# Sums of weighed ada chunks folded on VectorE over 32x32 block transposes, and copies of the bias rows issued from Pool's queue in the first MLP

## The chip, the cores and the metric

The kernel runs on one core of a Trainium2 chip. The metric is the device time of one execution in microseconds (us), as the median over runs. PE is TensorE, DVE is VectorE, ACT is ScalarE, POOL is GpSimd, and SP is SyncE, which here only issues DMAs.

## What is computed

Two transformer layers act on 256 latent tokens `x` and 256 context tokens `ctx`, with width D = 1024. Layer 0 mixes tokens by retention (4 heads, both directions, a gate per head), layer 1 by neighbourhood attention with a relative position bias `rpb`; each is followed by an MLP with squared ReLU and 4096 hidden units. Each layer takes six modulation vectors from the conditioning vectors `c` (latent) and `c_ctx` (context):

```
mod   = silu(c)    @ ada_w[i] + ada_b[i]       # 6 x 1024 numbers
mod_c = silu(c_ctx) @ ada_w[i] + ada_b[i]
sh1, sc1, g1, sh2, sc2, g2 = split(mod, 6)
h = x * (1 + sc1) + sh1                        # shift and scale, before each mixer and MLP
x = layer_norm(alpha * x + g1 * mixer(h))      # g: the gate on the branch
```

All data are 32-bit floats. The matrix `ada_w` has 2 x 1024 x 6144 elements, so the products are small beside the rest, but their weights are 48 MB.

## The kernel before

**The big products** are three matmuls each: ACT rounds a weight chunk `raw` to `hi`, DVE makes `lo = raw - hi`, activations are split in the same way (`hTh`/`hTl`, `oh`/`ol`), and PE adds `hi*hi + lo*hi + hi*lo` in PSUM. Weight chunks of 512 KB come over SP's queue into a ring of four buffers. Results are named after their stage: `pq`, `pv`, `pS`, `pg`, `pw` are the projections, scores, gates and output products of the retention heads, and `p` those of the MLPs and of layer 1.

**The retention heads** run one after the other (h = 0 to 3). The last stage of a head multiplies its gated output by the output weights: for each half of the columns and for each of four token tiles, 12 matmuls into `pw`. Each token tile is turned by PE, copied by ACT into `oh`, and its remainder `ol` is made by DVE (`to_oT`), two tiles ahead of the stage's first half and two within it. DVE then makes `acc = pw * G`, and POOL or DVE adds `acc` to the residual `R`. Scratch tiles (`acc`, `far`, `neg` and others) come from one ring of eight buffers, `scr`.

**The modulation vectors** for later use come from a background stream, the generator `bg_stream` (line 508). It goes through ten parts of `ada_w` (layer, which half of the layer w, and part 0 and 1 for shift and scale, 2 for the gate), with eight chunks (n = 0 to 7) of 512 KB for each part, called `rawa`. A call of `bg()` at certain places of the retention heads and of the MLPs advances the stream by one chunk, and loads the chunk after it into the same ring of four buffers that the weights use. The first part goes through PE. For the other nine, DVE weighs the rows (`weigh`, line 479): the element of silu(c) on each partition times the chunk, added up over chunks in `strips` (layer 0: 128x512 for each of latent and context) or `acc` (layer 1: 128x1024). What is left is a sum over the 128 partitions:

- `fold_rows` (line 488) adds the partitions up on PE: matmuls of 256 columns with a weight tile of 32 columns (`onecol`, in tile `misc`) that holds a column of ones, so that the sums land in one row of a group of 32 partitions. Layer 0 does so six times (in two halves for each of three parts, for latent and context), layer 1 six times (two with latent and context, four with latent alone).
- `ada_row` (line 445) adds the bias, which two DMAs on SP's queue (`ada_bias`, line 422) have spread over the partitions in `brow`.
- For shift and scale, `ada_columns` (line 451) turns the row into columns with two matmuls against the constant `sel`, and DVE writes them to `mods` with two adds. This is deferred to the next call of `bg()` by the list `due`. For the gate, POOL writes the row to DRAM (`grow`), from where it is later read on all partitions.

**The bias rows** of layer 1: `outside` (line 380) stores the negated bias in DRAM (`rpb_neg`) and fills the DRAM array `rpb_rows` with a large number by 14 DMAs of 256 KB (`far`) on SP's queue. `shifted_biases` (line 391) then copies for each of 64 grid columns a window of 16 columns from `rpb_neg` into `rpb_rows`, in 79 DMAs on SP's queue. They are read by POOL's DMAs in layer 1's attention. `outside` is called in head 2 of the retention.

**What sets the order**: a tile scheduler places the instructions of an engine by their dependences and priorities; each engine then runs its list strictly in order, and an instruction that waits holds all that stand behind it.

Of the kernel before, what the change touches and what calls it, by code (L numbers as in the profile page):

```python
# [39 lines left out]
def make_consts():  # L40
    f = np.float32
    parts = []

    def add(name, a):
        off = sum(p.shape[1] for p in parts)
        CONST_COLS[name] = (off, a.shape[1])
        parts.append(a.astype(f))

    p = np.arange(P)
    add("ident", np.eye(P))  # L50
    sel = np.zeros((P, 8))
    for j in range(4):
        for i in range(2):
            sel[32 * j + i, 2 * j + i] = 1.0
    add("sel", sel)

    sel4 = np.zeros((P, 4))
    for j in range(4):
        for i in range(2):
            sel4[32 * j + i, i] = 1.0  # L60
    add("sel4", sel4)
    inv = f(1.0) / (f(10000.0) ** (np.arange(0, 128, 2, dtype=f) / f(128.0)))
    row = np.arange(NLAT // GRID_W).astype(f)
    col = np.arange(GRID_W).astype(f)
    inv2 = inv[p % 64]
    for nm, ax in (("row", row), ("col", col)):
        ang = (ax[None, :] * inv2[:, None]).astype(f)
        add("cos" + nm, np.cos(ang))
        sg = np.where(p < 64, 1.0, -1.0)[:, None]
        add("sin" + nm, np.sin(ang) * sg)  # L70
    base = np.concatenate(parts, axis=1)
    d = (np.arange(384)[None, :] - 128 - p[:, None]).astype(f)
    return np.ascontiguousarray(base, dtype=f), np.ascontiguousarray(d)
# [36 lines left out]
def kernel(  # L110
# [184 lines left out]

    NC0 = P + 8 + 4
# [18 lines left out]
    cT = cpool.tile([P, KC, 16, 2], F32, tag="cT", name="cT")  # L317
    scol = cpool.tile([P, 2, KC], F32, tag="scol", name="scol")
    bcol = cpool.tile([P, 2, KC], F32, tag="bcol", name="bcol")
    lns = dram.tile([64, P], F32, tag="lns", name="lns")  # L320

    def first_columns():
# [16 lines left out]
    def ln_rows():  # L339
        rows = scr("rows")[:, :P]  # L340
        sp.dma_start(out=rows[0:32, :], in_=ln_g.rearrange("l i (k p) -> (l i k) p", p=P))
        sp.dma_start(out=rows[32:64, :], in_=ln_b.rearrange("l i (k p) -> (l i k) p", p=P))
        return rows

    def ln_columns(rows):

        pc = bank("pc")
        pe.transpose(pc[:, 0:64], rows[0:64, :], ident[0:64, 0:64])
        dve.tensor_copy(out=lnT[:].rearrange("p a b c k -> p (a b c k)"), in_=pc[:, 0:64])
        lsc = scr("lsc")  # L350
        pool.tensor_scalar_mul(out=lsc[0:64, :P], in0=rows[0:64, :], scalar1=ALPHA)
        pool.dma_start(out=lns[:], in_=lsc[0:64, :P])
# [38 lines left out]
    def shifted_biases(q):  # L391
        cs = min(max(q - 8, 0), GRID_W - 16)
        for b in range(2):
            c0, c1 = max(cs, HALFW * b), min(cs + 16, HALFW * (b + 1))
            if c0 < c1:
                src = rpb_neg[:, 4 : 4 + NRR, 15 - q + c0 : 15 - q + c1]
                sp.dma_start(out=rpb_rows[q][:, b, :, c0 - HALFW * b : c1 - HALFW * b], in_=src)


    pool.memset(onecol[:], 0.0)  # L400
# [19 lines left out]
        return raw  # L420

    def ada_bias(l, offs, nb):
        brow = smp.tile([P, 256], F32, tag="brow", name=nm("brow"), bufs=1)
# [24 lines left out]
        dve.tensor_add(out=row[p0:p1, :nb], in0=pr[p0:p1, 0:nb], in1=brow[p0:p1, :nb])  # L448
        return row

    def ada_columns(l, w, pr, row, nb, c0):

        ni = nb // P
        for i in range(ni):
            pe.matmul(
                pr[:, 256 + 8 * i : 264 + 8 * i],
                lhsT=row[:, i * P : (i + 1) * P],
                rhs=cv("sel"),
                start=True,
                stop=True,  # L460
            )
        m = mods[l, w]
        for s in range(2):
            src = pr[:, 256 : 256 + 8 * ni].rearrange("p (i s j t) -> p s j i t", i=ni, s=2, j=2)[:, s]
            dst = m[:, s, c0 : c0 + 2 * ni, :].rearrange("p (j i) t -> p j i t", i=ni)
            dve.tensor_scalar_add(out=dst, in0=src, scalar1=float(s))

    def on_pe(l, w, part):
        return (l, w, part) == (0, 0, 2)
# [10 lines left out]
    def weigh(acc, raw, t, k, first):  # L480
# [7 lines left out]
    def fold_rows(pr, js, nt, src):  # L488

        for t in range(nt):  # L490
            for i, j in enumerate(js):
                pe.matmul(
                    pr[32 * j : 32 * j + 32, 0:256],
                    lhsT=onecol[:, 1 - t : 33 - t],
                    rhs=src(t)[:, i * 256 : (i + 1) * 256],
                    start=(t == 0),
                    stop=(t == nt - 1),
                    tile_position=(0, 32 * j),
                )


    due = []

# [4 lines left out]
    def bg_stream():  # L508


        plan = []
        for l, w, part in (
            [(0, 0, 2), (0, 1, 0), (0, 1, 1), (0, 1, 2)]
            + [(1, 0, 0), (1, 0, 1), (1, 0, 2), (1, 1, 0), (1, 1, 1), (1, 1, 2)]
        ):
            sh, sc, g = 3 * w * D, (3 * w + 1) * D, (3 * w + 2) * D
            offs = (sh + 512 * part, sc + 512 * part) if part < 2 else (g, g + 512)
            for n in range(KC):
                plan.append((l, w, part, offs, n))
        nxt = bg_load(*plan[0])  # L520
        yield
        for step, (l, w, part, offs, n) in enumerate(plan):
            raw = nxt
            if step + 1 < len(plan):
                nxt = bg_load(*plan[step + 1])

            nt = 2 if l == 0 or (w == 0 and part < 2) else 1
            if n == 0:
                brow = ada_bias(l, offs, 256)
                row = None  # L530
            if on_pe(l, w, part):
                if n == 0:
                    pr = bank("pada")
                ada_mm(pr, n, 256, lambda j: raw[:, j // 2, (j % 2) * 256 : (j % 2 + 1) * 256])
                if n == KC - 1:
                    row = ada_row(pr, brow, 256)
            elif l == 0:
                for kk in range(2):
                    for t in range(nt):
                        weigh(spare(t), raw[:, kk, :], t, 2 * (n % 4) + kk, n % 4 == 0 and kk == 0)  # L540
                if n % 4 == 3:
                    yield
                    s = n // 4
                    pr = bank("pada")
                    fold_rows(pr, (2 * s, 2 * s + 1), nt, spare)
                    row = ada_row(pr, brow, 256, 64 * s, 64 * s + 64, row)
            else:
                if n == 0:
                    acc = slot(S_VL, [P, 2, D], F32, "acc")
                for t in range(nt):  # L550

                    dve.on = n == 0 and (w, part) == (0, 0)
                    weigh(acc[:, t], raw[:].rearrange("p a n -> p (a n)"), t, n, n == 0)
                    dve.on = False
                if n == KC - 1:
                    pr = bank("pada")
                    fold_rows(pr, range(4), nt, lambda t: acc[:, t])
                    row = ada_row(pr, brow, 256)
            if n == KC - 1:
                if part < 2:  # L560
                    due.append(lambda a=(l, w, pr, row, 256, 4 * part): ada_columns(*a))
                else:

                    for t in range(2 - l):
                        pool.dma_start(
                            out=grow[l, w][t].rearrange("(j c) -> j c", j=4), in_=row[t:P:32, :]
                        )
            yield

    bgs = bg_stream()  # L570
# [723 lines left out]
    for hf in range(2):  # L1294
# [9 lines left out]
        if hf == 0:  # L1304
# [894 lines left out]
```

## Time and profile before

| | |
|---|---|
| median of 3 runs | 1209.49 us (1208.81 to 1210.94) |
| the profiled execution | 1208.44 us |
| span of its instructions | 1206.4 us |
| PE busy | 1187.1 us (98%) |
| DVE busy | 822.0 us (68%) |
| ACT busy | 480.7 us (40%) |
| POOL busy | 211.5 us (18%) |

The profile is that of one execution on the chip. Times of rows are in us from the start of the span. Every operation of the kernel goes through one recorder, so nearly all rows show the line L89 (L84 in the changed kernel); the tiles tell them apart, as output `<-` inputs. A row of the timeline gives the start, the time taken, the engine, the operation, the tiles, the shape, and in square brackets the idle time before it with what ended it. A matmul of 128x512 is pipelined: it is shown as some 0.39 us long, but the next one starts 0.23 us after it. In float32, each matmul of the modulation vectors is two instructions.

### The profile page before, as it was taken

Reading aid. Unit: us, or ns where it says so; the run is one execution under the profiler, and the core shown is the slowest. Engines: PE = TensorE matmul, PEld = TensorE weight load, DVE = VectorE, ACT = ScalarE, POOL = GpSimd, SP = SyncE. Lnnn points to the kernel's source line nnn. Section 1 sums busy time; section 2 is a strip of 40 time slices with the busy share of each in tenths; the row PEclk is TensorE's granted clock in tenths of the full one; section 3 lists DMA queues with packets and bytes.
Section 4 is the critical chain, followed back from the end, with each engine's and each line's share of the span. In section 5 each row is a group of like instructions: output and inputs, shape, how many; then the busy total and the mean of one; then the engine's idle time right before and its main releaser. Section 6 shows DMA issues by size and latency. Waiting matters only on the chain.

```text
span 1206.4 us, 17989 instructions
## 1 busy us (share of the span) xinstructions
PE 1187.1 (98%) x6949; PEld 992.0 (82%) x6949; DVE 822.0 (68%) x1297; ACT 480.7 (40%) x809; POOL 211.5 (18%) x308
## 2 busy tenths in 40 slices
PE   7999999999999999999999999999999999999997
PEld 5777888888888889888888888889778878999886
DVE  3778857677686477668667675647566678787445
ACT  3562222323222246432123342227466665665341
POOL 1004501420340231000102000213345431000001
PEclk9999999999999999999999999999999999999999
DMA  9665443375543224336566566636344334666661
GB/s 305 220 227 193 139 143 109 105 264 127 134 146 122 73 70 132 114 105 192 176 195 205 186 213 207 218 106 189 90 143 131 94 127 158 192 210 198 239 207 38
DMA packets 147693, 194.29 MB, mean 161 GB/s; under 512 B 26960, under 2 KB 90760, under 8 KB 147608
## 3 DMA queue, kind: packets, MB, share of 16 engines
q1 hardware_dynamic: 141848, 181.08, 47.2%
q0 software_dynamic: 4608, 9.50, 2.8%
q10 hardware_dynamic: 1152, 2.57, 0.7%
q8 instruction: 54, 0.88, 0.3%
q14 instruction: 31, 0.25, 0.1%
HBM read 188.28 MB, written 5.75 MB: 161 GB/s over the span
## 4 chain that ended last, share of the span: by engine, by line
PE 86%; DVE 6%; ACT 3%; DMA 2%; issue 1%; POOL 1%; DVEq 0%; SPq 0%; ACTq 0%; POOLq 0%
PE p L89 41%; PE pq L89 7%; PE pv L89 7%; PE pw L89 6%; PE pg L89 6%; PE pn L89 5%; PE pnv L89 4%; PE pada L89 2%; PE po L89 2%; PE ppt L89 1%; DVE lo L89 1%; PE pS L89 1%; PE pqk L89 1%; DMA rawa<-in_ada_w_dram 1%; PE pav L89 1%
## 5 line engine op out<-in xcount | busy, mean ns | idle before, releaser
L89 DVE TENSOR_TENSOR lo<-raw,hi 128x1024 fp32r<-128x1024 f32 (+2 forms) x228 | 276.0, 1221 | 146.7 <-ACT hi L89 144.1
L89 ACT CAST hi<-raw 128x1024 fp32r<-128x1024 f32 (+2 forms) x228 | 232.7, 1033 | 347.8 <-PE p L89 178.0
L89 PE MATMUL p<-hi,hid 128*128 128x512 f32 (+1 forms) x832 | 242.3, 374 | 0.0
L89 PEld LDWEIGHTS p<-hi,hid 128*128 128x128 f32 x832 | 152.1, 188 | 28.9 <-issue 1.2
L89 PE MATMUL p<-hTh,lo 128*128 128x256 f32 (+1 forms) x512 | 167.4, 327 | 1.2 <-DVE lo L89 1.2
L89 PE MATMUL p<-hTh,hi 128*128 128x256 f32 (+1 forms) x512 | 168.1, 329 | 0.3 <-ACT hTh L89 0.3
L89 PE MATMUL p<-hTl,hi 128*128 128x256 f32 (+1 forms) x512 | 167.3, 327 | 0.3 <-DVE hTl L89 0.3
L89 PE MATMUL p<-lo,hid 128*128 128x512 f32 (+1 forms) x416 | 155.3, 373 | 0.0
L89 POOL TENSOR_TENSOR R<-R,acc 128x512 f32<-128x512 f32 x40 | 67.8, 1707 | 299.9 <-DVE acc L89 299.7
L89 PEld LDWEIGHTS p<-hTh,lo 128*128 128x128 f32 x512 | 96.4, 188 | 10.4 <-DVE lo L89 1.6
L89 PEld LDWEIGHTS p<-hTh,hi 128*128 128x128 f32 x512 | 96.3, 188 | 10.3 <-issue 1.2
L89 PEld LDWEIGHTS p<-hTl,hi 128*128 128x128 f32 x512 | 96.4, 188 | 9.4 <-DVE hTl L89 0.8
L89 DVE SCALAR_TENSOR_TENSOR acc<-rawa,scol,acc 128x1024 f32<-128x1024 f32 x56 | 71.1, 1282 | 31.3 <-DMA rawa<-in_ada_w_dram 31.0
L89 PEld LDWEIGHTS p<-lo,hid 128*128 128x128 f32 x416 | 78.4, 188 | 13.6
L89 DVE SCALAR_TENSOR_TENSOR strips<-rawa,scol,strips 128x512 f32<-128x512 f32 x84 | 70.1, 886 | 3.0 <-DMA rawa<-in_ada_w_dram 3.0
L89 ACT CAST hid<-r 128x256 fp32r<-128x256 f32 (+1 forms) x64 | 32.0, 500 | 69.7 <-DVE r L89 69.7
L89 POOL TENSOR_TENSOR rstd<-rstd,misc 128x1 f32<-128x1 f32 x28 | 18.8, 671 | 213.9 <-DVE rstd L89 211.9
L89 ACT ACTIVATE s<-s,mn 128x512 f32<-128x512 f32 x64 | 45.5, 712 | 26.2 <-DVE mn L89 26.2
L89 DVE TENSOR_TENSOR hid<-r,hid 128x256 fp32r<-128x256 f32 (+1 forms) x64 | 34.6, 541 | 25.8 <-ACT hid L89 25.6
L89 PE MATMUL pg<-hi,hTh 128*128 128x512 f32 x128 | 51.3, 401 | 0.0
L89 PE MATMUL pw<-hi,oh 128*128 128x512 f32 x128 | 51.2, 400 | 0.0
L89 PE MATMUL pv<-hi,hTh 128*128 128x512 f32 x128 | 50.3, 402 | 0.0
(232 smaller groups left out, 2266.7 us busy)
## 6 DMA issues: line engine op xcount, KB each, us to landing
raw<-in_mlp_w_dram SPq DMA_DIRECT2D x128, 512.0 KB
rawa<-in_ada_w_dram SPq DMA_DIRECT2D x80, 512.0 KB
raw<-in_ret_w_in_dram SPq DMA_DIRECT2D x42, 512.0 KB
raw<-in_nat_w_in_dram SPq DMA_DIRECT2D x24, 512.0 KB
rawq<-in_ada_w_dram SPq DMA_DIRECT2D x16, 512.0 KB
raw<-in_ret_w_o_dram SPq DMA_DIRECT2D x16, 512.0 KB
bias<-rpb_rows POOLq DMA_DIRECT2D x32, 128.0 KB, 2.7
raw<-in_nat_w_o_dram SPq DMA_DIRECT2D x8, 512.0 KB
```

The costliest lines, as they stand in the source:

```text
L89: r = f(*args, **kwargs)
```

## The change

1. The sum over partitions moves from PE to DVE. `folded` is a DVE reduction over blocks of 32 columns with a transposition of 32x32 blocks: from 128x512 it leaves 128x16 (from 128x1024, 128x32), in which partition 32*q + i of column b holds the sum, over the 32 partitions of quadrant q, of the old column 32*b + i. The last sum over the four quadrants is a matmul with the constant `fold` (a 128x32 matrix of four identities), which also brings the columns to their places. `fold_rows` and `sel` go.
2. `ada_columns` is four matmuls with 16 or 8 columns and one DVE add, with the bias as columns (`acol`). These come at the start of the kernel through three more DMAs into the tile of the layer norm's rows and the transposition of 112 rows in place of 64. The `brow` loads of nine parts go.
3. `ada_gate` is one matmul of 32x64 or 32x32, a DVE transposition of 32x32 blocks, an add of the bias (loaded by POOL's DMA), and POOL's DMAs to `grow`. It is deferred by `due` too.
4. `outside` is called in the first MLP, behind its context part, and the 79 copies of `shifted_biases` are issued by POOL.
5. In the gates of tiles 2 and 3 of a head, `bg()` is called at tile 2 alone, and in the head's output stage once more, at tile 1 of the first half.

```
+    def folded(red, acc, t, c0, n):
+        dve.tensor_reduce(
+            out=red[:, t, c0 // 32 : (c0 + n) // 32], in_=acc.rearrange("p (b i) -> p b i", i=32),
+            axis=mybir.AxisListType.X, op=ALU.add, apply_transpose=True,
+        )
+    def ada_columns(l, w, red, c0, nt):
+        pr = bank("pada")
+        for j in range(4):
             pe.matmul(
-                pr[:, 256 + 8 * i : 264 + 8 * i],
-                lhsT=row[:, i * P : (i + 1) * P],
-                rhs=cv("sel"),
+                pr[32 * j : 32 * j + 32, 0 : 8 * nt],
+                lhsT=cv("fold"),
+                rhs=red[:, :nt].rearrange("p t (k j) -> p j (t k)", j=4)[:, j],
...
+        dve.tensor_add(out=mods[l, w][:, :, c0 : c0 + 4, :],
...
+    def ada_gate(l, w, red, nt):
...
+        pool.dma_start(out=bias, in_=ada_b[l][g : g + D].rearrange("(b i) -> b i", i=32))
+        pr = bank("pada")
+        pe.matmul(
+            pr[0:32, 0 : 32 * nt], lhsT=cv("fold"), rhs=red[:, :nt].rearrange("p t b -> p (t b)"),
...
+        dve.transpose(out=tot, in_=pr[0:32, 0 : 32 * nt])
+        dve.tensor_add(
...
                 if n % 4 == 3:
                     yield
-                    s = n // 4
-                    pr = bank("pada")
-                    fold_rows(pr, (2 * s, 2 * s + 1), nt, spare)
-                    row = ada_row(pr, brow, 256, 64 * s, 64 * s + 64, row)
+                    for t in range(nt):
+                        folded(red, spare(t), t, 512 * (n // 4), 512)
...
                 if n == KC - 1:
-                    pr = bank("pada")
-                    fold_rows(pr, range(4), nt, lambda t: acc[:, t])
-                    row = ada_row(pr, brow, 256)
+                    for t in range(nt):
+                        folded(red, acc[:, t], t, 0, D)
...
-                sp.dma_start(out=rpb_rows[q][:, b, :, c0 - HALFW * b : c1 - HALFW * b], in_=src)
+                pool.dma_start(out=rpb_rows[q][:, b, :, c0 - HALFW * b : c1 - HALFW * b], in_=src)
...
-        if h == 2:
-            outside()
...
             pool.tensor_mul(out=gs[:, t, :], in0=sg[:], in1=gs[:, t, :])
-            bg()
+            if t == 2:
+                bg()
...
                     if half == 0 and t < 2:
                         to_oT(t + 2)
-                    elif t % 2 == 1:
+                    if t % 2 == 1:
                         bg()
...
             hid += hts
+            outside()
```

Three places show how the engines' lists move. On PE, in head 1, stands the first event that turns a part into columns; `pg` is the gate projection. Before:

```order
L89 MATMUL pg_1754<-hi_1659,hTh 128x512
L89 MATMUL pg_1754<-lo_1660,hTh 128x512
L89 MATMUL pg_1754<-hi_1659,hTl 128x512
L89 MATMUL pada_1687<-cst_81,row_1291 128x8 x2
L89 MATMUL pg_1793<-hi_1557,hTh 128x512
```

The same place of the changed kernel:

```order
L84 MATMUL pg_1749<-hi_1658,hTh 128x512
L84 MATMUL pg_1749<-lo_1659,hTh 128x512
L84 MATMUL pg_1749<-hi_1658,hTl 128x512
L84 MATMUL pada_1775<-red_1121,cst_82 32x16 x4
L84 MATMUL pg_1788<-hi_1556,hTh 128x512
```

The event keeps its place, with four narrow matmuls for two; the matmuls from `strips` and `acc` into `pada`, which stood elsewhere in PE's list, are gone from it.

On DVE, this is the first half of the output stage of head 0, behind the last `gs` (gated output of tile 3). Before:

```order
L89 TENSOR_TENSOR lo_1193<-raw_1190,hi_1192 128x1024
L89 TENSOR_TENSOR ol_1086<-pT_1128,oh_1085 128x4x128
L89 TENSOR_TENSOR lo_1199<-raw_1196,hi_1198 128x1024
L89 TENSOR_TENSOR ol_1086<-pT_1141,oh_1085 128x4x128
L89 TENSOR_TENSOR lo_1205<-raw_1202,hi_1204 128x1024
L89 TENSOR_TENSOR acc_1221<-pw_1208,G_993 128x512
L89 TENSOR_TENSOR ol_1086<-pT_1224,oh_1085 128x4x128
L89 TENSOR_TENSOR acc_1244<-pw_1231,G_993 128x512
L89 TENSOR_TENSOR ol_1086<-pT_1247,oh_1085 128x4x128
```

And of the changed kernel:

```order
L84 TENSOR_REDUCE red_1121<-strips_119 128x16
L84 TENSOR_TENSOR lo_1191<-raw_1188,hi_1190 128x1024
L84 TENSOR_TENSOR ol_1092<-pT_1132,oh_1091 128x4x128
L84 TENSOR_SCALAR strips_118<-rawa_1252,scol 128x512
L84 TENSOR_SCALAR strips_119<-rawa_1252,scol 128x512
L84 SCALAR_TENSOR_TENSOR strips_118<-rawa_1252,scol,strips_118 128x512
L84 TENSOR_TENSOR lo_1197<-raw_1194,hi_1196 128x1024
L84 TENSOR_TENSOR ol_1092<-pT_1145,oh_1091 128x4x128
L84 SCALAR_TENSOR_TENSOR strips_119<-rawa_1252,scol,strips_119 128x512
L84 TENSOR_TENSOR lo_1203<-raw_1200,hi_1202 128x1024
L84 TENSOR_TENSOR acc_1219<-pw_1206,G_999 128x512
L84 TENSOR_TENSOR ol_1092<-pT_1222,oh_1091 128x4x128
```

A reduction now stands between the two `lo` of this half's weights, and the weighing of a new chunk stands between the `ol` of consecutive token tiles; three more of its instructions (of `rawa_1336`) follow ahead of the last `ol`. In before, the weighing stood behind all four `ol`, in the second half of the stage.

On POOL, this is the way from the end of the retention layer (`rstd`, the layer norm's statistics) to the first MLP's second product, whose results are added to the residual `R`. Before:

```order
L89 TENSOR_TENSOR R_102<-R_102,acc_3821 128x512
L89 TENSOR_TENSOR rstd_3845<-rstd_3845,misc 128x1
L89 TENSOR_TENSOR R_101<-R_101,acc_4992 128x512
L89 TENSOR_TENSOR R_101<-R_101,acc_4995 128x512
L89 TENSOR_TENSOR R_102<-R_102,acc_4998 128x512
```

The end of the copies in the changed kernel:

```order
L84 DMA rpb_rows<-rpb_neg 32x7x14
L84 DMA rpb_rows<-rpb_neg 32x7x1
L84 DMA rpb_rows<-rpb_neg 32x7x15
L84 DMA rpb_rows<-rpb_neg 32x7x16 x24
L84 TENSOR_TENSOR R_102<-R_102,acc_4964 128x512
L84 TENSOR_TENSOR R_102<-R_102,acc_4967 128x512
```

All 79 copies stand ahead of the first add of the MLP's results, behind one wait for the 14 fills; SP's list has lost them in heads 2 and 3, and has the fills in the first MLP.

More of the change, by code (lines that the diff above doesn't have):

```diff
@@ L50, in make_consts @@
     add("ident", np.eye(P))
[L51 to L55, printed above, removed]
     sel4 = np.zeros((P, 4))
@@ L70, in make_consts @@
         add("sin" + nm, np.sin(ang) * sg)
+    add("fold", p[:, None] % 32 == np.arange(32)[None, :])
     base = np.concatenate(parts, axis=1)
@@ L347, in ln_columns @@
         pc = bank("pc")
-        pe.transpose(pc[:, 0:64], rows[0:64, :], ident[0:64, 0:64])
+        pe.transpose(pc[:, 0:112], rows[0:112, :], ident[0:112, 0:112])
         dve.tensor_copy(out=lnT[:].rearrange("p a b c k -> p (a b c k)"), in_=pc[:, 0:64])
+        ab = pc[:, 64:112].rearrange("p (i s k) -> p i s k", i=3, s=2)
+        for a in range(2):
+            dve.tensor_scalar_add(out=acol[:, :, a], in0=ab[:, :, a], scalar1=float(a))
         lsc = scr("lsc")
@@ L422, in ada_bias @@
     def ada_bias(l, offs, nb):
-        brow = smp.tile([P, 256], F32, tag="brow", name=nm("brow"), bufs=1)
+        brow = scr("brow")
         ab = ada_b[l]
@@ L459, in ada_columns @@
                 start=True,
                 stop=True,
+                tile_position=(0, 32 * j),
             )
[L462 to L466, printed above, removed]
+        dve.tensor_add(
+            out=mods[l, w][:, :, c0 : c0 + 4, :],
+            in0=(
+                pr[:, 0:16].rearrange("p (t s k) -> p s k t", t=2, s=2)
+                if nt == 2
+                else pr[:, 0:8].rearrange("p (s k) -> p s k", s=2).unsqueeze(3).broadcast_to([P, 2, 4, 2])
+            ),
+            in1=acol[:, COLUMNS.index((l, w)), :, c0 : c0 + 4].unsqueeze(3).broadcast_to([P, 2, 4, 2]),
+        )
@@ new lines, in ada_gate @@
+    def ada_gate(l, w, red, nt):
+        tmp = scr("gate")[0:32, :]
+        bias, tot, row = tmp[:, 0:32], tmp[:, 64 : 64 + 32 * nt], tmp[:, 128 : 128 + 32 * nt]
+        g = (3 * w + 2) * D
+        pool.dma_start(out=bias, in_=ada_b[l][g : g + D].rearrange("(b i) -> b i", i=32))
+        pr = bank("pada")
+        pe.matmul(
+            pr[0:32, 0 : 32 * nt], lhsT=cv("fold"), rhs=red[:, :nt].rearrange("p t b -> p (t b)"),
+            start=True, stop=True, tile_position=(0, 0),
+        )
+        dve.transpose(out=tot, in_=pr[0:32, 0 : 32 * nt])
+        dve.tensor_add(
+            out=row.rearrange("p (t i) -> p t i", t=nt), in0=tot.rearrange("p (t i) -> p t i", t=nt),
+            in1=bias.unsqueeze(1).broadcast_to([32, nt, 32]),
+        )
+        for t in range(nt):
+            pool.dma_start(
+                out=grow[l, w][t].rearrange("(b i) -> b i", i=32), in_=row[:, 32 * t : 32 * t + 32]
+            )
@@ L536, in bg_stream @@
                     row = ada_row(pr, brow, 256)
-            elif l == 0:
+                    for t in range(2):
+                        pool.dma_start(
+                            out=grow[l, w][t].rearrange("(j c) -> j c", j=4), in_=row[t:P:32, :]
+                        )
+                yield
+                continue
+            if n == 0:
+                red = smp.tile([P, 2, 32], F32, tag="red", name=nm("red"), bufs=2)
+            if l == 0:
                 for kk in range(2):
```

36 lines of the change are left out of this document (13 added, 23 removed).

## The prediction

> **What bounds the kernel now.** The page's busy times and slices come first, then what PE waits for, then two long windows.
>
> ```profile
> span 1206.4 us, 17989 instructions
> PE 1187.1 (98%) x6949; PEld 992.0 (82%) x6949; DVE 822.0 (68%) x1297; ACT 480.7 (40%) x809; POOL 211.5 (18%) x308
> PE   7999999999999999999999999999999999999997
> ```
>
> ```profile
> PE pc L89 <- DMA cst<-in_consts_dram: 4.8, 1, 4.8
> PE pc L89 <- DMA brow<-in_ada_b_dram: 2.2, 1, 2.2
> PE p L89 <- DVE lo L89: 1.2, 2, 0.8
> ```
>
> ```profile
> 120.00:440.00 320.00, 320.00 (x1476) 261.42 (x1475) 222.46 (x330) 86.68 (x123) 77.94 (x70) 1.00 0.45 136
> 470.00:830.00 360.00, 359.78 (x1737) 298.56 (x1738) 237.24 (x283) 119.57 (x168) 34.17 (x39) 1.00 0.53 171
> ```
>
> (Columns of the waits: total us, times, longest. Of the windows: length, then busy time of PE, PE's loads, DVE, ACT, POOL; granted clock, DMA share, GB/s.) PE is busy in every slice. Its two longest waits are at the start, for constants; the next cause has 1.2 us in all. From 120 to 440 (the retention heads) and from 470 to 830 (MLP, layer 1's projections, second MLP's product) PE has no hole, at a granted clock of 1.00. So an instruction taken off PE there is time saved, as long as no other engine makes PE wait. DVE is 68% busy, thus second, and is where this change puts work. All edits of the stream lie in these two windows.
>
> **What leaves PE.** I read the price of an event from the starts around it, since busy times overlap. First a fold of layer 0, then one of layer 1 with latent and context, one with latent alone, and one turn into columns:
>
> ```profile
> 129.01 0.39 PE L89 MATMUL pw<-hi,ol 128*128 128x512 f32 x1
> 129.33 1.06 PE L89 MATMUL pada<-strips,misc 128*32 128x256 f32 x8
> 130.31 0.50 PE L89 MATMUL pw<-hi,oh 128*128 128x512 f32 x1
> 130.66 0.40 PE L89 MATMUL pw<-lo,oh 128*128 128x512 f32 x1
> ```
>
> ```profile
> 590.00 0.39 PE L89 MATMUL p<-hi,hid 128*128 128x512 f32 x1
> ...
> 591.32 0.50 PE L89 MATMUL p<-hi,hid 128*128 128x512 f32 x1
> 591.66 0.40 PE L89 MATMUL p<-lo,hid 128*128 128x512 f32 x1
> ```
>
> ```profile
> 792.77 0.39 PE L89 MATMUL p<-hi,hid 128*128 128x512 f32 x1
> ...
> 793.65 0.50 PE L89 MATMUL p<-hi,hid 128*128 128x512 f32 x1
> 793.99 0.39 PE L89 MATMUL p<-lo,hid 128*128 128x512 f32 x1
> ```
>
> ```profile
> 195.47 0.39 PE L89 MATMUL pg<-hi,hTl 128*128 128x512 f32 x1
> 195.70 0.51 PE L89 MATMUL pada<-cst,row 128*128 128x8 f32 x4
> 196.06 0.49 PE L89 MATMUL pg<-hi,hTh 128*128 128x512 f32 x1
> 196.38 0.40 PE L89 MATMUL pg<-lo,hTh 128*128 128x512 f32 x1
> ```
>
> A step of 512 columns is 0.23 (195.47 to 195.70). The fold of layer 0 takes 129.01 to 130.31, 1.30, and the step behind it is 0.35. Less two steps of 0.23 it costs 1.65 - 0.46 = 1.19. Likewise layer 1 with two token sets: 1.32 + 0.34 - 0.46 = 1.20; with one: 0.88 + 0.34 - 0.46 = 0.76; the turn into columns: 0.59 + 0.32 - 0.46 = 0.45. The counts follow from the instructions:
>
> ```profile
> L89 PE MATMUL pada<-acc,misc x64: 379/379/403, 590.3 to 793.3; 128*32 128x256 f32 x64
> L89 PE MATMUL pada<-strips,misc x48: 379/379/403, 129.3 to 394.1; 128*32 128x256 f32 x48
> ```
>
> 48 at 8 an event are 6 folds of layer 0; 64 are 2 at 16 and 4 at 8. Six parts of shift and scale give 6 turns. Removed: 6 x 1.19 + 2 x 1.20 + 4 x 0.76 + 6 x 0.45 = 15.3 us.
>
> **What comes to PE.** Six turns of the new form (four matmuls, in four column groups that run side by side) and three gates (one matmul). From the folds, four instructions in a row on one column group cost 1.19 and two cost 0.76, so an instruction of 256 columns costs 0.22 and 0.33 stays for the change to a small shape and back. Two instructions of 16 to 64 columns are between 0 and 2 x 0.22. I take 0.5 for an event, nearest to the 0.45 of the old turn with 8 columns: 9 x 0.5 = 4.5, with bounds of 3.0 and 6.9. **PE's net is -10.8 us** (-8.4 to -12.3).
>
> **What comes to DVE.** No row of this trace is a reduction over transposed blocks. The nearest are elementwise operations of the same size:
>
> ```profile
> L89 DVE TENSOR_TENSOR acc<-pw,G 128x512 f32<-128x512 f32 x32 | 21.7, 682 | 11.1 <-PE pw L89 11.1
> L89 DVE TENSOR_TENSOR R<-xn,gb 128x1024 f32<-128x1024 f32 x8 | 9.8, 1220 | 0.0
> ```
>
> ```profile
> L89 DVE TENSOR_TENSOR row<-pada,brow x13: 404/425/427, 95.2 to 793.8; 128x256 f32<-128x256 f32 x7, 64x256 f32<-64x256 f32 x6
> L89 DVE TENSOR_SCALAR mod<-pada x12: 153/157/167, 196.2 to 757.4; 128x8 f32<-128x8 f32 x12
> L89 DVE SCALAR_TENSOR_TENSOR strips<-rawa,scol,strips x84: 720/747/1784, 93.2 to 372.3; 128x512 f32<-128x512 f32 x84
> ```
>
> Twelve reductions of 128x512 at 0.68 and eight of 128x1024 at 1.22 are 17.9. Six adds into `mods` and three transpositions with add, at some 0.16 each, are 1.9. Twelve `row` adds (5.0) and twelve adds into `mods` (1.9) go. DVE gets about 13 us more, 835 of 1200. Spread out, this is hidden in DVE's idle 32%; it costs where DVE is ahead of PE by little. A reduction shorter than that gives nothing more, since PE's gain is counted already; as the upper bound I take four times the row, 2.7 and 4.9, since it brings 32 partitions together in a form that no row shows: that would be 54 us more on DVE, a rival below. [...]
>
> **Where DVE makes PE wait.** In head 0's output stage the margin is already gone:
>
> ```profile
> 114.70 2.35 DVE L89 TENSOR_TENSOR lo<-raw,hi 128x1024 fp32r<-128x1024 f32 x2
> 116.97 0.69 DVE L89 TENSOR_TENSOR ol<-pT,oh 128x512 fp32r<-128x512 f32 x1
> ...
> 119.36 0.68 DVE L89 TENSOR_TENSOR ol<-pT,oh 128x512 fp32r<-128x512 f32 x1
> ```
>
> ```profile
> 117.71 0.50 PE L89 MATMUL pw<-hi,ol 128*128 128x512 f32 x1 [0.27 <-DVE ol L89]
> ```
>
> PE waits 0.27 for the first `ol`. A token tile is 12 matmuls, 2.74 us, so PE needs the second, third and fourth `ol` at about 120.4, 123.1 and 125.9. In the new order one reduction (0.68) stands between the two `lo`: the first `ol` ends at 118.4, and PE waits 0.7 more. Then DVE meets the weighing of `rawa_1252`. Its buffer comes free with the first `lo`, at 115.9; 512 KB at the page's 161 GB/s are 3.3 us,
>
> ```profile
> DMA packets 147693, 194.29 MB, mean 161 GB/s; under 512 B 26960, under 2 KB 90760, under 8 KB 147608
> ```
>
> so it lands near 119.3, and three weighing instructions (0.7 each, by the row of 0.747 above), a `lo` (1.2) and the second `ol` (0.7) end at 123.2; PE, by then due at 121.1, waits 2.1. The third `ol` has 3.3 us of DVE work ahead of it (a weighing, a `lo`, an `acc`, itself) and PE gives 2.7: 0.5. The fourth has 3.6 against 2.7, less what the waits gave: 0.3. Together 3.6 us. The bounds are 0 (chunk there early, 0.5 for each weighing) and 7 (landing 3.5 later). Behind the wait for `rawa` stand `lo`, `ol` and `acc` alike, so everything on DVE is late with it. Heads 1 and 2 have the same list, but there the second `ol` is ready long before the stage needs it:
>
> ```profile
> 220.91 0.69 DVE L89 TENSOR_TENSOR ol<-pT,oh 128x512 fp32r<-128x512 f32 x1
> 225.42 0.68 DVE L89 TENSOR_TENSOR acc<-pw,G 128x512 f32<-128x512 f32 x1
> ```
>
> It ends at 221.6, and the first token tile's `acc` starts only at 225.4. The same sum gives 0.5 each there (0 to 3). In head 3 the add of the gate waits for POOL's load of the bias ahead of DVE's work for the layer norm: 0.3. Layer 1's reductions fall where DVE waits for `rawa` anyway: 0. **Given back: 4.9**, bounds 0 and 12.
>
> **Copies and fills.** In before, the copies stand on SP's queue between 269 and 335, in the window above in which PE has no hole. So taking them away gains 0. Now they stand on POOL:
>
> ```profile
> 588.05 5.05 POOL L89 TENSOR_TENSOR R<-R,acc 128x512 f32<-128x512 f32 x4 [126.56 <-DVE acc L89]
> ```
>
> ```profile
> L89 SPq DMA_DIRECT2D rpb_rows<-rpb_neg x79: 528/607/1703, 269.0 to 334.8; - x79
> L89 SPq DMA_DIRECT2D rpb_rows<-far x14: 320/502/1017, 250.5 to 260.1; - x14
> L89 POOL DMA_DIRECT2D bias<-rpb_rows x64: 565/582/662, 815.7 to 984.8; - x64
> ```
>
> POOL is idle for 126 us before 588, and its DMAs take 0.58 each to issue: 79 are 46 us. The fills took 10 us to issue and stand in the first MLP's first third, so I start the copies at about 507 and end them at 553. That hides under the idle time, with 35 us to spare, so 0; without that cover the first adds of the MLP would be late. The fills (14 of 256 KB on SP's queue, ahead of the MLP's weights) are 3.7 MB, 23 us at 161 GB/s beside a stage that moves 171 GB/s in the window above; SP's issues run a ring of four chunks ahead of PE: I cost them at 0, with 3 us as the upper bound. The start (three more small DMAs, 48 more columns to transpose): 0.1.
>
> **Sum.** -10.8 + 4.9 + 0.1 = -5.8 on the profiled execution of 1208.44, which lies 1.05 under the median of 1209.49. On the median that is **1203.7 us**.
>
> **Rivals.**
>
> *Full gain.* The chunk has landed before DVE comes to it, or the `ol` get ahead of the weighing in time; PE waits no more than now. For it: PE's waits for DVE are 2 us in all today. Against: the order. 1209.5 - 10.8 = 1198.7.
>
> *DVE's new order takes it all.* Landing 3.5 us later in heads 0 to 2 is 10 us of PE's wait: -10.8 + 10 + 0.4 = 1209, no change. For it: `lo`, `ol` and `acc` stand behind a DMA wait three times; against: the early `ol` of heads 1 and 2.
>
> *POOL's queue holds the MLP (slower).* If a copy costs more than (588 - 507) / 79 = 1.03 us on POOL, the `R` adds start late; `acc` buffers then stay taken in the ring of eight, DVE halts, then PE. At 1.3 us, POOL is 22 us late; less some 4 us of cover, 1203.7 + 18 = 1222. For it: a copy is 32x7 runs of 16 numbers, where a load of `bias` has runs of 128, and no row shows POOL at such short ones. Against: SP's 0.607 for the same copies, POOL's 0.58. [...]
>
> *A dear reduction (slower).* At four times the row, twelve reductions in the heads are 2.05 us longer each. If all are ahead of what PE waits for, 24 us: 1228. It decides from 0.68 + 8 / 12 = 1.4 us on, where the gain is half gone to it and the rest to the waits above. Against: DVE's idle time between heads' stages.
>
> **How the numbers follow.** Forecast (1200.5 to 1207) 0.56; full gain 0.22; no change 0.11; POOL's queue 0.05; dear reduction 0.06. A measurement tells about 0.2% (2.4 us) from no change, so faster means under 1207.1: 0.78; same 0.11; slower 0.11. The range takes the first two with their bounds: 1197.5 (PE's -12.3) to 1208 (stalls of 9).
>
> **What would show it.** PE's instructions on `strips` and `acc` gone and steps around a turn under 0.6: the -10.8. PE's waits for DVE `ol` in head 0 up to some 4 us: the giving back. A reduction of 128x512 near 0.7, one of 128x1024 near 1.2. POOL's copies over by 560, and its `R` adds at 580 or so not late. The prediction is wrong if a reduction takes over 1.4, a copy over 1.0, or if PE waits in the MLP for weights behind the fills.

## The result, and the profile after

| | before | changed |
|---|---|---|
| median of 7 runs | 1210.45 us (1208.22 to 1211.35) | 1206.88 us (1203.71 to 1208.76) |
| ratio, 95% interval | | 0.9971 (0.9961 to 0.9982) |
| profiled execution, its span | 1208.44, 1206.4 us | 1205.15, 1203.4 us |

The change gains 0.29% (0.18 to 0.39), about 3.6 us: faster, but little for the 15 us of matmuls that it takes off PE. The changed kernel's page, and two windows of it:

```profile
span 1203.4 us, 17830 instructions
PE 1176.1 (98%) x6867; PEld 986.4 (82%) x6867; DVE 825.5 (69%) x1307; ACT 477.8 (40%) x809; POOL 255.0 (21%) x390
```

```profile
120.00:440.00 320.00, 313.78 (x1427) 258.55 (x1428) 217.74 (x332) 85.52 (x121) 68.04 (x67) 0.99 0.37 119
...
470.00:830.00 360.00, 359.65 (x1732) 300.86 (x1733) 247.71 (x292) 119.39 (x174) 87.02 (x125) 1.00 0.61 185
```

PE lost 11.0 us of busy time, but the span only 3.0. The window of the MLP is still full. That of the heads, which had no hole, now has 6.2 us without PE, and its granted clock is 0.99 in place of 1.00. What PE waits for names it:

```profile
PE pw L84 <- DVE ol L84: 6.5, 4, 2.8
PE pc L84 <- DMA cst<-in_consts_dram: 4.7, 1, 4.7
PE p L84 <- DVE lo L84: 1.9, 3, 0.8
PE pc L84 <- DMA brow<-in_ada_b_dram: 1.5, 1, 1.5
```

To see where the time went, I took the same matmul in both traces (all of PE's instructions but those of `pada`, which are in the same number in both) and compared its start, changed less before:

| PE has reached (time in before) | difference, us | what lies between |
|---|---|---|
| end of head 0's gates (112) | -1.0 | start of the kernel |
| end of head 0's output stage (142) | +4.0 | one fold less, two waits, a slow stretch |
| end of head 1's (248) | +3.1 | two folds less, a wait of 1.4 |
| end of head 2's (354) | +1.4 | two folds less, a wait of 0.8 |
| first MLP (460) | +0.7 | one fold less, the gate's new event |
| behind the last fold of layer 1 (794) | -4.9 | six folds less, four turns, a gate |
| first product of the second MLP (1066) | -3.4 | a wait for `lo` |
| last matmul | -3.4 | |

Layer 1 gives what the folds cost. The retention layer gives all of its folds back and 1.7 us besides. Here is DVE in head 0's output stage in the changed kernel (some rows left out):

```profile
112.17 1.22 DVE L84 TENSOR_TENSOR lo<-raw,hi 128x1024 fp32r<-128x1024 f32 x1
113.30 0.70 DVE L84 TRANSPOSE_TENSOR_REDUCE red<-strips 128x16 f32<-128x512 f32 x1
113.93 1.18 DVE L84 TENSOR_TENSOR lo<-raw,hi 128x1024 fp32r<-128x1024 f32 x1
115.03 0.68 DVE L84 TENSOR_TENSOR ol<-pT,oh 128x512 fp32r<-128x512 f32 x1
117.13 1.94 DVE L84 TENSOR_SCALAR strips<-rawa,scol 128x512 f32<-128x512 f32 x2 [1.42 <-DMA rawa<-in_ada_w_dram]
...
120.79 0.68 DVE L84 TENSOR_TENSOR ol<-pT,oh 128x512 fp32r<-128x512 f32 x1
...
127.19 1.41 DVE L84 SCALAR_TENSOR_TENSOR strips<-rawa,scol,strips 128x512 f32<-128x512 f32 x2 [2.73 <-DMA rawa<-in_ada_w_dram]
```

DVE waits 1.42 for the first chunk with the second `ol` behind it, and 2.73 for the second chunk with the fourth `ol` behind it. PE there:

```profile
121.53 0.50 PE L84 MATMUL pw<-hi,ol 128*128 128x512 f32 x1 [1.85 <-DVE ol L84]
...
130.52 0.61 PE L84 MATMUL pw<-hi,ol 128*128 128x512 f32 x1 [2.80 <-DVE ol L84]
130.92 0.63 PE L84 MATMUL pw<-hi,oh 128*128 128x512 f32 x1
131.35 0.63 PE L84 MATMUL pw<-lo,oh 128*128 128x512 f32 x1
```

Behind the wait of 2.80 the matmuls are 0.63 long and 0.43 apart, where they were 0.39 and 0.23. The window shows the cause, a granted clock of 0.66 on the mean:

```profile
130.00:135.00 5.00, 4.48 (x13) 3.54 (x14) 5.00 (x7) 1.35 (x2) 2.45 (x2) 0.66 0.32 105
```

The trace's clock records put it at one half for 3.4 us. The nine steps behind this wait take 3.75 us, where the nine behind the wait of 1.85 take 2.16: 1.6 us on top of the wait. Behind the wait of 1.85 nothing of the kind happens.

### The profile page after: what moved, and what is told of

Same layout as the page of the kernel before. It is cut to its first block, busy times and chain, and to the rows that moved or that the text cites. A ratio compares the mean times of both kernels' runs of the same rounds, so it can differ in the third digit from the quotient of the medians.

```text
span 1203.4 us, 17830 instructions
## 1 busy us (share of the span) xinstructions
PE 1176.1 (98%) x6867; PEld 986.4 (82%) x6867; DVE 825.5 (69%) x1307; ACT 477.8 (40%) x809; POOL 255.0 (21%) x390
## 4 chain that ended last, share of the span: by engine, by line
PE 82%; DVE 8%; DMA 4%; issue 2%; ACT 2%; POOL 1%; SPq 0%; DVEq 0%; ACTq 0%; POOLq 0%
PE p L84 40%; PE pq L84 7%; PE pv L84 7%; PE pn L84 5%; PE pg L84 5%; PE pw L84 4%; PE pnv L84 4%; DMA rawa<-in_ada_w_dram 2%; DVE lo L84 2%; PE po L84 2%; PE ppt L84 2%; PE pS L84 1%; PE pqk L84 1%; PE pada L84 1%; PE pav L84 1%
## 5 line engine op out<-in xcount | busy, mean ns | idle before, releaser
L84 DVE SCALAR_TENSOR_TENSOR acc<-rawa,scol,acc 128x1024 f32<-128x1024 f32 x56 | 74.7, 1344 | 66.0 <-DMA rawa<-in_ada_w_dram 66.0
L84 POOL TENSOR_TENSOR R<-R,acc 128x512 f32<-128x512 f32 x40 | 63.2, 1596 | 209.9 <-DVE acc L84 209.8
L84 DVE SCALAR_TENSOR_TENSOR strips<-rawa,scol,strips 128x512 f32<-128x512 f32 x84 | 66.8, 830 | 9.8 <-DMA rawa<-in_ada_w_dram 9.7
L84 PE MATMUL pw<-hi,ol 128*128 128x512 f32 x128 | 51.0, 398 | 6.5 <-DVE ol L84 6.5
L84 PE MATMUL pw<-lo,oh 128*128 128x512 f32 x128 | 50.5, 394 | 0.0
```

Source lines behind the costliest of these rows:

```text
L84: r = f(*args, **kwargs)
```

## The experiments

My theory (A): the sums on DVE free the `strips` earlier, so the scheduler pulls the weighing of the next part into the output stage, ahead of `ol`; what PE then waits for is a chunk's DMA. Rivals: the new places of `bg()` do it (B), the moved copies (C), DVE's added work itself (D). All times are medians; ratios are to the kernel before, run beside each. The sets of runs were made on different chips, with medians of the kernel before from 1209.19 to 1210.45, so two kernels of different sets are compared by their ratios (0.001 is 1.2 us). Waits and half clock are those of the one profiled execution of each.

| kernel | us | ratio (95%) | PE's wait for `ol`, us | half clock in the heads, us |
|---|---|---|---|---|
| changed | 1206.88 | 0.9971 (0.9961 to 0.9982) | 6.5 | 3.4 |
| calls of `bg()` back | 1203.09 | 0.9953 (0.9939 to 0.9967) | 4.3 | 0 |
| copies back | 1212.46 | 1.0034 (1.0021 to 1.0046) | 11.8 | 3.4 + 6.8 |
| both back: sums alone | 1204.82 | 0.9968 (0.9948 to 0.9988) | 5.6 | 3.4 |
| before, `bg()` moved alone | 1208.77 | 0.9996 (0.9986 to 1.0006) | 0.5 | 0 |
| before, copies moved alone | 1210.52 | 1.0002 (0.9992 to 1.0012) | 1.0 | 0 |
| changed, DVE in order | 1196.91 | 0.9905 (0.9890 to 0.9921) | none | 0 |
| the same, copies back | 1203.46 | 0.9950 (0.9935 to 0.9964) | 1.2 | 6.8 |
| the same, reductions twice | 1197.33 | 0.9894 (0.9878 to 0.9909) | none | 0 |

### The calls of `bg()` back at their places

```
             pool.tensor_mul(out=gs[:, t, :], in0=sg[:], in1=gs[:, t, :])
-            if t == 2:
-                bg()
+            bg()
...
-                    if t % 2 == 1:
+                    elif t % 2 == 1:
```

> The changed kernel with the calls of bg() back at their old places (gates of tiles 2 and 3, none at tile 1 of the first half of the output stage). In the changed kernel's profile PE waits 6.5 us for ol and runs 1.65 us at half clock behind the longest of these waits. Theory A (DVE's list has the weighing of a chunk ahead of ol, since the reductions free the strips early): in this kernel's list two multiplications and an addition of a chunk still stand ahead of the first ol of head 0 and three more ahead of the fourth, so PE still waits 3 to 6 us for ol in head 0, under 1 us in heads 1 and 2; time 1203 to 1207, about 0.995 to 0.998 of before. Theory B (the place of the bg() calls makes the waits): PE waits under 0.5 us for ol, time 1199, 0.991 of before.

Measured: 1203.09, waits of 2.2 and 1.6 in head 0 and 0.5 in head 1, no half clock. As A had it: PE still waits for `ol` with the calls back, so their place does not make the waits. Whether it adds to the time is less sure: 2.2 us by the ratios, whose intervals overlap.

### The fills and copies back

```
-                pool.dma_start(out=rpb_rows[q][:, b, :, c0 - HALFW * b : c1 - HALFW * b], in_=src)
+                sp.dma_start(out=rpb_rows[q][:, b, :, c0 - HALFW * b : c1 - HALFW * b], in_=src)
...
+        if h == 2:
+            outside()
...
-            outside()
```

> The changed kernel with the fills and the 79 copies of the bias rows back in head 2 and on SP's queue. Theory A (the copies cost nothing in either place): the same time as the changed kernel within 1.5 us, 0.996 to 0.998 of before, PE's waits for ol 5 to 8 us. Rival C (the copies on POOL and the fills in the MLP take something, or SP's queue free of copies lets chunks come earlier): over 2 us to either side.

A's number fell, and rival C's "over 2 us" came true: 1212.46, 7.6 us slower than the changed kernel by the ratios, and slower than before. DVE and PE in head 2's output stage of this kernel:

```profile
323.74 0.69 DVE L84 TENSOR_TENSOR ol<-pT,oh 128x512 fp32r<-128x512 f32 x1
332.76 0.88 DVE L84 TENSOR_SCALAR strips<-rawa,scol 128x512 f32<-128x512 f32 x2 [8.33 <-DMA rawa<-in_ada_w_dram]
```

```profile
336.09 0.80 PE L84 MATMUL pw<-hi,ol 128*128 128x512 f32 x1 [4.82 <-DVE ol L84]
```

DVE waits 8.33 for one chunk, which SP issues at 328.82, behind 35 copies that begin at 305.16; PE idles 4.82 and then runs 6.8 us at half clock. So the copies matter where `ol` stands behind a chunk. This edit moves place and queue of the copies together; no run has them on SP's queue in the first MLP.

### DVE in program order where `ol` is made

```
                 us = take(2)
+                dve.on = half == 0
                 for t in range(4):
                     tok(t, half, us)
```

> The changed kernel with DVE held to program order in the first half of each output stage, so that all four ol stand ahead of the weighing; no instruction is added or removed. Theory A: PE's waits for ol fall from 6.5 to under 0.6 us, no stretch at half clock in the heads, about 8 us less than the changed kernel: 1199, 0.990 to 0.992 of before. Theory D (DVE simply has too much to do with 17.9 us of reductions): the waits only move to other tiles, time within 2 us of the changed kernel.

Measured: 1196.91, ratio 0.9905, with the same instructions. PE has no wait for `ol`, and the window of the heads is full again at a clock of 1.00, as in before:

```profile
120.00:440.00 320.00, 319.94 (x1472) 264.58 (x1471) 233.16 (x352) 89.97 (x129) 68.82 (x72) 1.00 0.37 119
```

That shows the order of DVE's list, and not its work, to be what the gain was lost to. The kernel is 12.3 us below before, and 8.0 below the changed one by the ratios.

### More for PE to do ahead of the wait

```
+            if (h, t, half) == (0, 3, 0):
+                for _ in range(8):
+                    pe.matmul(pw[:], lhsT=oh[:, 0, tsl(0)], rhs=us[0][0][:, 0, :], start=True, stop=True)
```

> The changed kernel with eight matmuls more (1.8 us, their result is overwritten) in head 0 ahead of token tile 3 of the first half, where PE idled 2.8 us before the half clock. Theory A with the half clock as a consequence of the idle time: idle falls to about 1.0, the nine matmuls behind it take 0.23 instead of 0.43 each, 1.65 us less than the changed kernel: 1205.2. Rival E (the half clock has another cause, such as the load on the whole chip at that time): the same half-clock stretch, time within 0.5 us of the changed kernel.

Inconclusive in time: 1205.65, ratio 0.9971 (0.9959 to 0.9984), not to be told from the changed kernel. The profiled execution is the longest of twelve, with 1211.77. In its profile the fourth `ol` came about 1 us later too, so PE idled 2.08 and not 1.0, and no half clock followed in head 0:

```profile
128.04 2.20 PE L84 MATMUL pw<-hi,oh 128*128 128x512 f32 x9
130.08 0.39 PE L84 MATMUL pw<-lo,oh 128*128 128x512 f32 x1
132.55 0.51 PE L84 MATMUL pw<-hi,ol 128*128 128x512 f32 x1 [2.08 <-DVE ol L84]
132.89 0.40 PE L84 MATMUL pw<-hi,oh 128*128 128x512 f32 x1
```

In head 2 of the same execution, PE idled 2.8 us for `ol`, and 3.4 us at half clock followed there. The other eleven executions have a mean granted clock of 0.998 or 0.999, like the kernel before, where the seven of the changed kernel have 0.995 to 0.997; one such stretch lowers the mean by 0.0014 (half of 3.41 us in a span of 1203). So the stretch was gone from most executions, which speaks against E, though the time doesn't show it.

### Each edit alone on the kernel before

The places of `bg()` alone (the edit of the change's fifth point, on the kernel before):

> The kernel before with nothing but the changed places of the bg() calls; the folds stay on PE, the copies in head 2 on SP's queue. Theory A: the folds on PE hold the strips until late, so that in DVE's list all four ol of head 0 still stand ahead of the weighing; PE's waits for ol under 1 us, time 1208 to 1211, 0.999 to 1.001 of before. Theory B (the place of the calls alone makes the waits): waits of 4 us and more, time 1213 or above.

The fills and copies alone (its fourth point):

> The kernel before with nothing but the fills and copies moved to the first MLP and POOL's queue; the folds stay on PE. Theory F (in the kernel before, the weights behind the copies arrive just in time for PE, so their move alone gives nothing): 1208 to 1210.5, 0.999 to 1.001 of before. Rival (the copies cost the kernel before several us too): 1204 or below.

1208.77 and 1210.52: neither does anything that can be measured, as expected. The sums alone (points 1 to 3):

> The changed kernel with both the calls of bg() and the fills and copies back at their old places: only the sums on DVE are left of the change. Theory F (the copies on SP's queue in head 2 set a time that the heads can't undercut once the folds are off PE; the calls of bg() cost a little): head 0 as with the calls back (PE waits about 4 us for ol), in head 2 PE waits 3 to 5 us more and runs some 3 to 7 us at half clock behind it: 1206 to 1211. Rival (the copies do harm only with the new places of the calls): 1202 to 1204.

1204.82, between the two ranges, so neither theory's time came: waits for `ol` of 2.5 us in head 0 (F had some 4) and 3.1 in head 2, and 3.4 us at half clock behind the latter, as F had it. (The mean granted clock of the five executions, 0.996 to 0.999, says that not all have this stretch.) The sums alone make PE wait for `ol`, so neither B nor C is needed for that. No edit but the sums gains by itself, and the edits do not add up. By the ratios, beside the sums, moving `bg()` takes 8.0 us (0.9968 to 1.0034) and moving the copies then gives 7.6 (1.0034 to 0.9971), or with the old places of `bg()` 1.8 (0.9968 to 0.9953), which the intervals do not tell from nothing.

### In order, with the copies back

The edits of the second and third experiment together.

> DVE in program order in the first half of the output stages, as in the kernel of 1196.9 us, and the fills and copies back in head 2 on SP's queue, which cost the changed kernel 5.6 us. Theory A (the copies only delay chunks, which cost only where ol stands behind a chunk): 1196 to 1198.5, no wait of PE for ol. Rival C (the copies on SP's queue hold the heads' weights too): 1202 or above.

A fell again, and rival C's range came true: 1203.46, 5.4 us lost by the ratios although no `ol` stands behind a chunk. SP, ACT and PE of this kernel in head 2, in a profiled execution of 1207.33, the longest of six:

```profile
297.32 26.27 SPq L84 DMA_DIRECT2D rpb_rows<-rpb_neg  x39
323.68 0.54 SPq L84 DMA_DIRECT2D raw<-in_ret_w_in_dram  x1
```

```profile
327.95 1.04 ACT L84 CAST hi<-raw 128x1024 fp32r<-128x1024 f32 x1 [6.99 <-DMA raw<-in_ret_w_in_dram]
```

```profile
329.53 0.50 PE L84 MATMUL pw<-hi,oh 128*128 128x512 f32 x1 [2.86 <-ACT oh L84]
```

and of before, SP and ACT:

```profile
308.84 13.83 SPq L89 DMA_DIRECT2D rpb_rows<-rpb_neg  x20
322.77 0.54 SPq L89 DMA_DIRECT2D raw<-in_ret_w_in_dram  x1
```

```profile
327.10 1.05 ACT L89 CAST hi<-raw 128x1024 fp32r<-128x1024 f32 x1 [0.43 <-DMA raw<-in_ret_w_in_dram]
```

In both, the weight chunk behind the copies is issued at about 323, since SP works through the copies at its own pace (39 in 26.27 us here, 20 in 13.83 in before: some 0.7 each). In before, ACT came to it 0.43 us too early, and its `oh` behind it was still in time. A kernel that has left its folds and waits behind arrives some 6 us earlier at the same place; ACT then waits 6.99, `oh` stands behind `hi`, PE idles 2.86 and 1.24 us, and 6.8 us at half clock follow. The copies cost nothing in before because PE was just slow enough.

### The reductions twice

In the kernel with DVE in order, `folded(red, spare(t), t, 512 * (n // 4), 512)` stands twice.

> DVE in program order in the first half of the output stages, and each of the twelve reductions of the retention heads done twice (same result): 8.3 us more of DVE. Theory A (DVE's idle time hides the reductions): 1196.5 to 1199, PE's waits for DVE not above 1 us more. Theory D (the reductions' time on DVE is on the path): up to 8 us more, 1203 to 1205.

Ratio 0.9894 against 0.9905: 8.3 us more on DVE do not show. Rival D is out for the reductions of the heads, with DVE in this order; the eight of layer 1 were not doubled.

### Two idle times made by hand

In the kernel with DVE in order, the line of `to_oT` that makes `ol` is repeated:

```
+            for _ in range({(1, 3): 9, (2, 3): 6}.get((h, t), 1)):
                 dve.tensor_sub(out=ol[:, :, tsl(t)], in0=pv_, in1=oh[:, :, tsl(t)].bitcast(F32))
```

> DVE in program order in the first half of the output stages, where the fourth ol is made nine times in head 1 and six times in head 2 (same result), at 0.61 us each. PE has 1.65 us of slack there, so it idles about 3.2 us in head 1 and 1.4 us in head 2. Theory A (an idle time of PE of nearly 3 us is followed by some 3.4 us at half clock, one of 2 us or less is not): nine matmuls behind the idle time of head 1 take 0.43 us each, those of head 2 take 0.23; time 1196.9 + 4.6 + 1.65 = 1203. Rival E (the half clock doesn't hang on the idle time): all matmuls at 0.23, 1201.5.

It told nothing: 1197.94, no such idle time, since the scheduler put matmuls of the second half into the gap. With PE held to program order there as well (`pe.on = h > 0` in the stage, eight and six times):

> As the kernel with the two idle times, but with PE in program order too in the output stages of heads 1 and 2, so that no matmul of the second half can step into the gap; the fourth ol is made eight times in head 1 and six times in head 2 at 0.72 us each, less 1.65 us of slack: PE idles about 3.4 us in head 1 and 2.0 in head 2. Theory A (a long idle time is followed by about 3.4 us at half clock, a short one is not): a half-clock stretch in head 1 alone; 1196.9 + 5.4 + 1.65 = 1204. Rival E: no such stretch, 1202.3.

1205.55, ratio 0.9963 (0.9949 to 0.9977). PE behind the two waits:

```profile
230.29 0.79 PE L84 MATMUL pw<-hi,ol 128*128 128x512 f32 x1 [3.25 <-DVE ol L84]
230.88 0.63 PE L84 MATMUL pw<-hi,oh 128*128 128x512 f32 x1
```

```profile
335.61 0.52 PE L84 MATMUL pw<-hi,ol 128*128 128x512 f32 x1 [1.80 <-DVE ol L84]
335.95 0.61 PE L84 MATMUL pw<-hi,oh 128*128 128x512 f32 x1
336.36 0.63 PE L84 MATMUL pw<-lo,oh 128*128 128x512 f32 x1
```

Both are followed by 3.4 us at half clock, also the one of 1.80, where waits of 1.85 and 2.22 elsewhere were not. The half clock does follow from the idle time (rival E is out), but the length of the wait alone does not decide; the last section sets the waits beside a grid of windows.

## Why the prediction was right, and what was mis-sized

The time is inside the range, though only 0.1 us from its upper end, and on the side forecast; the forecast of -5.8 us was too much by 2.2. That the error is no larger is in part luck, since two terms were off in opposite directions: PE's net by 1.0 and what is given back by 3.5.

1. **What leaves and comes to PE: right.** The instructions on `strips` and `acc` are gone. The new turn costs less than the 0.5 I took:

```profile
198.31 0.39 PE L84 MATMUL pg<-hi,hTl 128*128 128x512 f32 x1
198.63 0.26 PE L84 MATMUL pada<-red,cst 128*32 128x16 f32 x8
198.82 0.50 PE L84 MATMUL pg<-hi,hTh 128*128 128x512 f32 x1
199.16 0.39 PE L84 MATMUL pg<-lo,hTh 128*128 128x512 f32 x1
```

0.51 + 0.34 - 0.46 = 0.39, and so the nine events are 3.5 and not 4.5; PE's net is -11.8, where -10.8 was forecast.

2. **The price on DVE: right.** The reductions take what the rows of elementwise work said (0.68 and 1.22):

```profile
L84 DVE TRANSPOSE_TENSOR_REDUCE red<-acc 128x32 f32<-128x1024 f32 x8 | 9.7, 1226 | 0.0
L84 DVE TRANSPOSE_TENSOR_REDUCE red<-strips 128x16 f32<-128x512 f32 x12 | 8.2, 694 | 0.0
```

This is the first row of this operation in the case. That DVE's idle time hides those of the heads is shown, for DVE in program order, by doing them twice (ratio 0.9894 against 0.9905). DVE's busy time rose by 3.5 us and not by 13: the work that comes and goes is as counted, but the weighing into `strips`, which the change leaves as it is, took 5.8 us less, and other rows changed by up to 3.5 either way; the runs do not show why.

3. **What is given back: the right mechanism, mis-sized.** The term was 4.9. By the profile's idle times it is 6.2 of longer waits (6.5 less the 0.27 of before) and 1.6 of half clock, 7.8 in all. The prices of events were read from start to start; read so, the four waiting steps are 2.25, 3.19, 1.65 and 1.01 us where 0.23 is usual. That is 7.2 us too long, where before had 0.4, and with the half clock the term is 8.4. The step that failed is "The fourth has 3.6 against 2.7, less what the waits gave: 0.3". It took the second chunk, `rawa_1336`, as landed, and so counted DVE's work alone. SP issued it only at 122.16, when the first chunk's last weighing had ended (121.39 + 0.73), and it landed at 127.1. DVE waited 2.73 us for it, PE 2.80, and then came the half clock, which the heads of before could not show, since PE had no step there above 0.65 us from start to start. For the first chunk I had asked when its buffer comes free and when it lands; the second chunk needed the same two questions. The second `ol` cost 1.85 (forecast 2.1); the first and the third cost nothing (forecast 0.7 and 0.5), since DVE was early there. The first `ol` was ready at 115.7 and not at 118.4: the start had gone 1.0 faster, and ACT was not held up by a weight chunk ahead of this `ol`, for which it had waited 1.83 us in before. Heads 1 and 2 gave 1.4 and 0.8 (forecast 0.5 each).

4. **The copies: right against before, and too short.** POOL did them as forecast, long before its next work:

```profile
L84 POOL DMA_DIRECT2D rpb_rows<-rpb_neg x79: 592/592/720, 499.2 to 547.2; - x79
```

```profile
591.83 7.99 POOL L84 TENSOR_TENSOR R<-R,acc 128x512 f32<-128x512 f32 x4 [44.05 <-DVE acc L84]
```

(0.592 each, from 499 to 548; POOL waits 44 us for its next add, and PE's window of the MLP is full. Nothing of the rival on POOL's queue shows.) "So taking them away gains 0" holds for the kernel before. But it was asked of the wrong kernel: with the folds gone, the copies at their old place and on SP's queue would have taken 7.6 us by the ratios.

5. The rest is -1.0 at the start, where PE's waits for constants vary between executions (4.6 to 5.0 us for `cst` and 1.4 to 2.4 for `brow` over the profiles of all kernels), and +0.9 in the second MLP, where PE waits for `lo` a little more than in the one profile of before. The latter stands in the profile of the kernel with only the copies moved too, whose time is that of before; I can't tell whether it belongs to the change, and leave it open. Together, -11.8 + 8.4 - 1.0 + 0.9 = -3.5, against the -3.4 of PE's last matmul. (The window from 470 to 830 holds the first MLP and the start of layer 1's projections; the second MLP begins only at 1032.)

## What to carry to other kernels

When work is taken off the engine that bounds the kernel, ask of every engine's new list what now stands ahead of the small instruction that the bound engine waits for, and for each DMA among it when its buffer comes free; each engine runs its list in order, so the wait is the DMA's and not the work's (in head 0, DVE's 2.73 us for a chunk became 2.80 of PE's for `ol`). A cover that is just long enough (ACT's wait for the chunk behind the copies was 0.43 us in before) is used up as soon as the kernel gets faster, so test an edit that does nothing alone together with the others. And an idle time of PE can cost more than its length: the one of 2.80 us was followed by 3.4 at half clock, which cost 1.6 more.

## What the runs showed of the hardware

**The half-clock stretches lay on a grid of 3.413 us.** In the six profiles with a half-clock stretch in the heads, each stretch is 3.413 us long or twice that (in the changed kernel it starts at 130.763, and the one at the end at 1199.135), and its start lies a whole number of such steps ahead of the half-clock stretch at the end of the same execution: 313.0 (changed), 316.0 and 256.0 (copies back), 254.0 (sums alone), 253.0 (more for PE), 255.0 (in order, copies back), 284.0 and 253.0 (two idle times). So in these profiles the stretches keep to a grid that is not tied to the wait. I divided each gap between matmuls (from 0.23 us behind the start of the last one, where the next starts over 0.43 us after it) by that grid, in all traces from 100 to 460 us:

| idle of PE in one window of 3.41 us at full clock | the next window |
|---|---|
| 2.57, 2.75, 2.84, 2.91, 2.96, 3.25, 3.41 | half clock |
| 2.04 | full clock |
| 1.96 | half clock |
| 0.09 to 1.73 (52 windows) | full clock |

Where the stretch is twice as long, PE idled 0.9 or 1.2 us more in its first window. In this table the border lies near 2 us, some 60% of a window; 1.96 and 2.04 are on the wrong sides of each other, and the ends of matmuls are known no better than that. It fits that the wait of 2.22 us (calls of `bg()` back) cost nothing more, since it lay across two windows (1.61 and 0.77), and that the one of 1.80 (two idle times, PE in order) cost 1.6 us more (1.96 in one window). What sets this border, no run shows.

**POOL issued the DMAs of many short runs at about the price of long ones.** 79 copies of up to 32x7 runs of 16 numbers took 0.592 us each (median) to issue on POOL in the changed kernel, where the same copies took 0.607 on SP's queue in before, and POOL's loads of `bias` with runs of 128 numbers 0.582.
